# Ordering the loads of a background weight preparation behind the stores of y

## The chip, the core and the metric

The kernel runs on one core of a Trainium2 chip. The metric is the device time of one execution in microseconds (us). Five engines work side by side, each taking its own instructions in order: PE (TensorE, matrix products), DVE (VectorE), ACT (ScalarE), POOL (GpSimd) and SP (SyncE), which in this kernel does nothing but issue DMAs, all of them. They meet through semaphores.

## What is computed

One decoder layer on a sequence of 2048 tokens of width 1024, in float32. In the reference, shortened:

```
u = rmsnorm(x, norm_mix)
z = u @ w_in                                  # 1024 -> 5392
aq, ak, av, gq, gk, gv, g_low, za, zg = split(z)
y_att = sliding_window_attention(rope(aq), rope(ak), av, sinks)      # 16 heads, 2 kv heads, window 128
log_g = log_sigmoid(g_low @ w_gate_up + b_gate) / 16
o     = gated_linear_attention(gq, gk, gv, log_g)                    # 4 heads, chunks of 64
y = concat(y_att * silu(za), rmsnorm(o, gla_norm) * silu(zg)) @ w_out    # 2048 -> 1024
h = x + y
h = h + sigmoid(rmsnorm(h, ple_norm) @ w_ple_gate) * (p @ w_ple_proj)
return rmsnorm(h, final_norm)
```

## The kernel before

Each float32 operand is split into a high and a low part, and a product is three passes of PE: high by high, high by low, low by high (`gemm`, L83).

**First phase** (L126 to L734). It runs in two halves of 1024 tokens. A half begins with a section over its eight blocks of 128 tokens: keys, values and the low-rank gate input (`section_a`), and one behind it the first block of GLA values (`v_block`). Then come four rounds `i`, one GLA head each: eight `v_block`s (in round 0 they have been done in the section), two pairs of `qk_block`s, eight `gla_tile`s; and behind them attention for two, one, one and no groups of four heads, each with eight `att_tile`s and four `za_block`s. Round 3 has no attention. `load_w` brings the weights of each block; in the first half it converts them (ACT copies the high part, POOL subtracts, L286 and L288) and stores the parts, in the second half it loads the stored parts (`wh`, `wl`, L278 and L279).

Every tile ends in a store to the array `yts` (called y below), from `oy` by attention (L480) and from `oyg` by GLA (L587).

The tails of these tiles are generators in a list `chains`. `tick()` advances each of them by one step; it is called behind each block, and `run_chain` runs a tile's first part, ticks and appends the tile.

**The right operands.** The second phase (L739 to the end) multiplies y by `w_out` in two passes, and the normalised result by `w_ple_gate`, by a scheme of seven products in place of eight on blocks of a 2 by 2 cut. Its right operands are seven combinations of each pass's weight blocks, each split in high and low. `right_operands` (L595) makes them while the first phase runs, as one of the chains, in 48 units (3 passes, 4 × 4 blocks). A unit takes four loads of 64 KB of raw rows (`rb`, L605), four differences on DVE (`tm`, by `diff`, L104), two copies on ACT (`th`, L621), two subtractions on POOL (L622) and four stores to `tds` (L624). A unit's loads stand in the code two units ahead of its differences. All of it lives in the nine buffers of the pool `rawp`, tag `raw`.

In round 3 of half 1, behind the `v_block`s, the pools of keys, values and raw rows are closed, the pool `tpr` takes their place (its tiles wait for the buffers they overlap) and the first three of the seven operands `T` are loaded (L122).

**What sets the order.** The program is written in one order, but a scheduler arranges each engine's instructions by its own model of time: among those that are ready it takes the one that stands first in the code. So an instruction that has nothing to wait for may be issued far ahead of its place in the code. A load of raw rows waits for a free buffer of `rawp` and nothing else.

Of the kernel before, what the change touches and what calls it, by code (L numbers as in the profile page):

```python
# [19 lines left out]
P = 128  # L20
# [18 lines left out]
def hybrid_block_kernel(  # L39
# [86 lines left out]
    with ExitStack() as p1:  # L126
# [181 lines left out]
        def tick():  # L308
            for c in list(chains):
                if next(c, True):  # L310
                    chains.remove(c)

        def spawn(c):
            chains.append(c)
# [94 lines left out]
        def att_tile(half, g, wq, lt, szas):  # L409
            kv = g // 2  # L410
            t = half * HT + lt
            ps = pt("acc")
            tok_gemm(ps, wq, lt, 0, 256)
            q = w1("q", shape=(P, 4, 64))
            act.activation(q, ps[:, 0:256].rearrange("p (h d) -> p h d", h=4), AF.Copy)
            rope(q, 4, t)
            stk = w2("stk", F32R, (P, 4, 2, 64))
            split(stk[:, :, 0, :], stk[:, :, 1, :], q)
            yield
            tp = pt("t", dtype=F32R)  # L420
            for j in range(4):
                pe.transpose(tp[:, j * P:(j + 1) * P], stk[:, j].rearrange("p a d -> p (a d)"), identr)
            qT = w2("qT", F32R, (P, 4, P))
            act.activation(qT, tp.rearrange("p (h n) -> p h n", h=4), AF.Copy)
            yield
            sp = pt("s", (P, 4, 256), bufs=1)
            win = slice(lt * P, lt * P + 256)
            for j in range(4):
                pe.matmul(sp[:, j, :], qT[:, j, :], kT[:, kv, 0, win], start=True, stop=False)
                pe.matmul(sp[:, j, :], qT[:, j, :], kT[:, kv, 1, win], start=False, stop=True)  # L430
            s = w2("s", F32, (P, 4, P))
            act.activation(s, sp[:, :, P:256], AF.Copy)
            um = umask.unsqueeze(1).broadcast_to([P, 4, P])
            if t == 0:
                dve.copy_predicated(s, um, negc.unsqueeze(2).broadcast_to([P, 4, P]))
            else:
                dve.copy_predicated(s, um, sp[:, :, 0:P])
            hsl = slice(4 * g, 4 * g + 4)
            sm = wk.tile([P, 6, 4], F32, name="sm", tag="sm", bufs=3)
            mx, ng, es, su, dn = (sm[:, i, :] for i in range(5))  # L440
            dve.tensor_reduce(out=mx, in_=s, op=ALU.max, axis=AX.X)
            dve.scalar_tensor_tensor(ng, mx, -1.0, nsk[:, hsl], op0=ALU.mult, op1=ALU.min)  # L442
            dve.tensor_tensor(es, ng, nsk[:, hsl], op=ALU.subtract)
            act.activation(es, es, AF.Exp)
            for j in range(4):
                act.activation(s[:, j, :], s[:, j, :], AF.Exp, bias=ng[:, j:j + 1], accum_out=su[:, j:j + 1])  # L446
            dve.tensor_tensor(dn, su, es, op=ALU.add)
            dve.reciprocal(dn, dn)
            dve.scalar_tensor_tensor(s, s, 0.5, dn.unsqueeze(2).broadcast_to([P, 4, P]),
                                     op0=ALU.mult, op1=ALU.mult)  # L450
            yield
            yield
            tp = pt("t")
            for j in range(4):
                pe.transpose(tp[:, j * P:(j + 1) * P], s[:, j, :], ident)
            pq = kvp.tile([P, 4, 512], F32R, name="pq", tag="pq", bufs=1)
            split(pq[:, 0, :], pq[:, 1, :], tp)
            pmb = pmask.unsqueeze(1).broadcast_to([P, 4, P])
            for i in range(2):
                pool.tensor_tensor(pq[:, 2 + i, :].rearrange("p (h n) -> p h n", h=4),  # L460
                                   pq[:, i, :].rearrange("p (h n) -> p h n", h=4), pmb, op=ALU.mult)
            yield
            yield
            po = pt("o")
            vp = vs[:, lt, kv].rearrange("p a d -> p (a d)")
            vq = vd[:, lt, kv].rearrange("p a d -> p (a d)")
            pe.matmul(po, vp, pq[:, 0, :], start=True, stop=False)
            pe.matmul(po, vp, pq[:, 1, :], start=False, stop=False)
            pe.matmul(po, vq, pq[:, 2, :], start=False, stop=False)
            pe.matmul(po, vq, pq[:, 3, :], start=False, stop=True)  # L470
            pv = po.rearrange("p (a b n) -> p a b n", a=2, b=2)
            ot = w1("ot", shape=(P, 2, P))
            act.activation(ot[0:64], pv[64:128, :, 0, :], AF.Copy)
            act.activation(ot[64:128], pv[0:64, :, 1, :], AF.Copy)
            dve.tensor_tensor(ot[0:64], ot[0:64], pv[0:64, :, 0, :], op=ALU.add)
            dve.tensor_tensor(ot[64:128], ot[64:128], pv[64:128, :, 1, :], op=ALU.add)
            oy = w1("oy", shape=(P, 2, P))
            l2 = lt % 4
            dve.tensor_tensor(oy, ot, szas[lt // 4][:, :, l2 * P:(l2 + 1) * P], op=ALU.mult)
            nc.sync.dma_start(yts[t][:, 2 * g:2 * g + 2, :], oy)  # L480


        def gla_gates(half, h, sub, res):
# [65 lines left out]
        def gla_tile(half, h, wz, lt, ops):  # L549
            t = half * HT + lt  # L550
            if t > 0:
                sd = w1("sd")
                dve.tensor_scalar(sd, st[:, h, :], dall[:, h, t - 1, 1:2], dall[:, h, t, 0:1],
                                  op0=ALU.mult, op1=ALU.mult)
                sh = w2("sh", F32R, (P, 2, 256))
                split(sh[:, 0], sh[:, 1], sd)
            yield
            kt, at, qq, vv = ops[lt]
            ps = pt("acc")
            tok_gemm(ps, wz, lt, 0, 256)  # L560
            m = w1("m")
            act.activation(m, ps[:, 0:256], AF.Tanh, scale=0.5)
            dve.scalar_tensor_tensor(m, m, 1.0, ps[:, 0:256], op0=ALU.add, op1=ALU.mult)  # L563
            pool.tensor_tensor(m, m, gn, op=ALU.mult)
            pk = pt("o")
            mm3(pk[:, 0:256], kt, vv, True, True)
            if t > 0:
                dve.tensor_tensor(st[:, h, :], pk[:, 0:256], sd, op=ALU.add)
            else:
                dve.tensor_copy(st[:, h, :], pk[:, 0:256])  # L570
            po = pt("o")
            if t > 0:
                mm3(po[:, 0:256], qq, sh, True, False)
            mm3(po[:, 0:256], at, vv, t == 0, True)
            y = w1("y")
            ss = small.tile([P, 1], F32, name="ss", tag="ss", bufs=4)
            act.activation(y, po[:, 0:256], AF.Square, accum_out=ss)
            rs = rms_scale(ss, 256)
            dve.scalar_tensor_tensor(y, po[:, 0:256], rs, m, op0=ALU.mult, op1=ALU.mult)
            yield  # L580
            yield
            tq = pt("t")
            for j in range(2):
                pe.transpose(tq[:, j * P:(j + 1) * P], y[:, j * P:(j + 1) * P], ident)
            oy = w1("oyg", shape=(P, 2, P))
            act.activation(oy, tq[:, 0:256].rearrange("p (a n) -> p a n", a=2), AF.Copy)
            nc.sync.dma_start(yts[t][:, 8 + 2 * h:10 + 2 * h, :], oy)  # L587

        def run_chain(c):
            next(c)  # L590
# [4 lines left out]
        def right_operands():  # L595
            units = [(ps_, k, c) for ps_ in range(3) for k in range(4) for c in range(4)]

            def piece(name, dtype=F32):
                return rawp.tile([P, 2 * SW], dtype, name=name, tag="raw")[:, 0:512].rearrange("p (b n) -> p b n", b=4)

            def load(ps_, k, c):
                r = piece("rb")

                for i, (kk, a) in enumerate(((0, 1), (0, 0), (1, 0), (1, 1))):
                    nc.sync.dma_start(r[:, i], srcs[ps_][(k + 4 * kk) * P:(k + 4 * kk + 1) * P,  # L605
                                                         512 * a + c * P:512 * a + c * P + P])
                return r

            rs_ = [load(*u) for u in units[:2]]
# [1 line left out]
            for n, (ps_, k, c) in enumerate(units):  # L611
# [15 lines left out]
                if n + 2 < len(units):  # L627
                    rs_.append(load(*units[n + 2]))
                yield
                if n % 3 == 0:  # L630
                    yield

        A_COLS = [(C_AK, 256), (C_GL, 16)]
# [18 lines left out]
        for half in range(2):  # L652
            if half > 0:
                carry_kv()
                spawn(right_operands())
            wv = load_w([(C_GV, 256)])
            vt, gates = {}, {}
            for s_ in range(HT + LAG):
# [16 lines left out]
                if s_ >= LAG:  # L675
                    v_block(wv, vt, s_ - LAG)
                    tick()

            for i in range(4):
                if i > 0:  # L680
# [7 lines left out]
                        tick()  # L688
                if half == 1 and i == 3:

                    kvs.close()
                    p2p["tpr"] = p2r.enter_context(tc.tile_pool(name="tpr", bufs=1, side="right", reuse_waits="tile"))
                    T = [None] * 7
                    load_T(0, ORDER[:3], T)
# [389 lines left out]
```

## Time and profile before

| | us |
|---|---|
| median of 3 runs | 1932.47 |
| lowest and highest | 1930.56, 1933.31 |
| the profiled execution | 1929.69 |
| span of the profiled execution (first to last instruction) | 1927.6 |
| PE busy | 1828.3 (95% of the span) |
| DVE busy | 1224.1 (64%) |
| ACT busy | 962.7 (50%) |
| POOL busy | 697.9 (36%) |
| DMA queue of SP | 324.70 MB, 52.2% of what 16 DMA engines could be busy |
| mean granted clock of PE | 0.981 of full speed |

Times in the profile are counted from the first instruction of the span. A share over the whole span mixes stages with different limits, so the stretches are what is to be read. Matmuls are pipelined and their ends modelled, so a busy PE may still hide gaps that are too short to see. POOL's spans are rough. Idle time of an engine matters only where the engine that sets the end waits for it.

### The profile page before, as it was taken

How to read it: one execution, taken by the hardware profiler on the slowest of the kernel's cores; microseconds unless marked ns; L12 is line 12 of the kernel's file. 1: busy time of each engine (PE TensorE's matmuls, PEld its weight loads, DVE VectorE, ACT ScalarE, POOL GpSimd, SP SyncE). 2: the span in 40 equal slices, each digit the busy share in tenths (PEclk: the TensorE clock that was granted, in tenths of full speed). 3: DMA queues.
4: the chain of work that ended last, by engine and by line, in shares of the span. 5: the costliest groups of instructions: out<-in, count | busy, mean ns of one | idle time of the engine just before them, and what ended most of it. 6: DMA issues, size and time to landing. Idle time of an engine off the chain costs nothing. (4 is left out here: it accounts for less than half of the span.)

```text
span 1927.6 us, 32806 instructions
## 1 busy us (share of the span) xinstructions
PE 1828.3 (95%) x11297; PEld 1626.3 (84%) x11297; DVE 1224.1 (64%) x2663; ACT 962.7 (50%) x2598; POOL 697.9 (36%) x916
## 2 busy tenths in 40 slices
PE   6999999999998888988999999999899999998997
PEld 6989898998998778778898998998788888786886
DVE  6455775475457776657774474475666666766875
ACT  5554665466456565546563464465422234453543
POOL 5452554443526678554332232232200001112322
PEclk9999999999999889999999999999999999999999
DMA  8332442423417998996232231335586876894542
GB/s 278 123 97 80 148 145 78 154 90 130 136 43 227 265 285 248 268 277 184 79 105 77 83 102 58 105 100 185 170 301 192 313 257 209 287 351 145 177 138 92
DMA packets 326741, 326.78 MB, mean 170 GB/s; under 512 B 23136, under 2 KB 259824, under 8 KB 326320
## 3 DMA queue, kind: packets, MB, share of 16 engines
q1 hardware_dynamic: 326576, 324.70, 52.2%
q8 instruction: 89, 1.46, 0.3%
q14 instruction: 76, 0.62, 0.1%
HBM read 186.08 MB, written 138.54 MB: 168 GB/s over the span
## 5 line engine op out<-in xcount | busy, mean ns | idle before, releaser
L85 PE MATMUL acc<-wh,uth 128*128 128x256 f32 (+1 forms) x1664 | 481.3, 290 | 15.1 <-DVE m L563 7.7
L86 PE MATMUL acc<-wl,uth 128*128 128x256 f32 (+1 forms) x1664 | 476.0, 286 | 0.9 <-DMA wl<-wd 0.8
L87 PE MATMUL acc<-wh,utl 128*128 128x256 f32 (+1 forms) x1664 | 475.6, 286 | 0.0
L85 PEld LDWEIGHTS acc<-wh,uth 128*128 128x128 f32 x1664 | 320.4, 193 | 26.7 <-DVE m L563 9.0
L86 PEld LDWEIGHTS acc<-wl,uth 128*128 128x128 f32 x1664 | 320.1, 192 | 6.1 <-DMA wl<-wd 1.5
L87 PEld LDWEIGHTS acc<-wh,utl 128*128 128x128 f32 x1664 | 320.2, 192 | 1.9
L460 POOL TENSOR_TENSOR pq<-pq,pmask 128x512 fp32r<-128x512 f32 x128 | 175.8, 1391 | 387.8 <-ACT pq L67 382.1
L85 PE MATMUL acc<-uth,wh 128*128 128x512 f32 x512 | 205.8, 402 | 3.8 <-DVE m L563 2.7
L87 PE MATMUL acc<-uth,wl 128*128 128x512 f32 x512 | 203.3, 397 | 1.0 <-DMA wl<-wd 1.0
L86 PE MATMUL acc<-utl,wh 128*128 128x512 f32 x512 | 203.8, 398 | 0.0
L768 PE MATMUL acc<-T,c 128*128 128x512 f32 (+1 forms) x344 | 135.0, 394 | 5.0 <-ACT u L823 4.8
L769 PE MATMUL acc<-T,c 128*128 128x512 f32 (+1 forms) x344 | 135.0, 392 | 0.0
L770 PE MATMUL acc<-T,c 128*128 128x512 f32 (+1 forms) x344 | 134.4, 393 | 0.0
L446 ACT ACTIVATE s<-s,sm 128x128 f32<-128x128 f32 x256 | 99.7, 391 | 51.6 <-DVE sm L442 51.3
L85 PEld LDWEIGHTS acc<-uth,wh 128*128 128x128 f32 x512 | 97.5, 190 | 26.0 <-DVE m L563 4.0
L87 PEld LDWEIGHTS acc<-uth,wl 128*128 128x128 f32 x512 | 97.2, 190 | 23.8 <-DMA wl<-wd 1.7
L288 POOL TENSOR_TENSOR wl<-raw,wh 128x512 fp32r<-128x512 f32 (+1 forms) x82 | 109.9, 1370 | 20.2 <-ACT wh L286 10.3
L853 POOL TENSOR_TENSOR ssh<-ssh 128x1 f32<-128x1 f32 x16 | 4.0, 250 | 312.5 <-ACT junk L852 312.5
L86 PEld LDWEIGHTS acc<-utl,wh 128*128 128x128 f32 x512 | 97.3, 190 | 18.9
L768 PE MATMUL o<-T,c 128*128 128x512 f32 (+1 forms) x252 | 98.7, 392 | 1.1 <-DVE xt L107 0.9
L769 PE MATMUL o<-T,c 128*128 128x512 f32 (+1 forms) x252 | 98.0, 389 | 0.0
L770 PE MATMUL o<-T,c 128*128 128x512 f32 (+1 forms) x252 | 97.9, 389 | 0.0
(288 smaller groups left out, 4382.4 us busy)
## 6 DMA issues: line engine op xcount, KB each, us to landing
T<-td SPq DMA_DIRECT2D x84, 512.0 KB, 9.0
wd<-wh SPq DMA_DIRECT2D x20, 1024.0 KB, 5.6
wd<-wl SPq DMA_DIRECT2D x20, 1024.0 KB, 6.4
wh<-wd SPq DMA_DIRECT2D x80, 256.0 KB, 5.4
wl<-wd SPq DMA_DIRECT2D x80, 256.0 KB, 5.6
raw<-in_w_in SPq DMA_DIRECT2D x68, 256.0 KB, 5.6
y<-yts SPq DMA_DIRECT2D x64, 256.0 KB, 6.1
td<-th SPq DMA_DIRECT2D x48, 256.0 KB, 3.0
```

The source lines that it names most:

```text
L85: pe.matmul(ps, lhs_h(k), rhs_h(k), start=(k == 0), stop=False)
L86: pe.matmul(ps, lhs_h(k), rhs_l(k), start=False, stop=False)
L87: pe.matmul(ps, lhs_l(k), rhs_h(k), start=False, stop=(k == nk - 1))
L288: eng.tensor_tensor(wl[:, ks_, 0:n], raw[:, :, 0:n], wh[:, ks_, 0:n], op=ALU.subtract)
L446: act.activation(s[:, j, :], s[:, j, :], AF.Exp, bias=ng[:, j:j + 1], accum_out=su[:, j:j + 1])
L460: pool.tensor_tensor(pq[:, 2 + i, :].rearrange("p (h n) -> p h n", h=4), pq[:, i, :].rearrange("p (h n) -> p h n", h=4), pmb, op=ALU.mult)
L768: pe.matmul(ps, c[:, 0, k, :], t[:, 0, k, sl], start=(first and k == 0), stop=False, skip_group_check=more)
L769: pe.matmul(ps, c[:, 0, k, :], t[:, 1, k, sl], start=False, stop=False, skip_group_check=more)
L770: pe.matmul(ps, c[:, 1, k, :], t[:, 0, k, sl], start=False, stop=(k == 3), skip_group_check=more)
L853: pool.tensor_tensor(ss[:, 0:1], ss[:, 0:1], ss[:, 1:2], op=ALU.add)
```

## The change

It gives the loads of raw rows a place in SP's queue. The instruction of the latest store of y is kept in `pace[0]`, and each unit's four loads are traced under `tc.issue_after(pace[0])`, which adds an order without a semaphore: on the engine of that store (SP) these loads come behind it. The chain is started behind the loop of half 1's section instead of at the start of half 1, it takes an empty tick after every sixth unit instead of every third, and an assert states that it has ended when its pool is closed.

```diff
@@ att_tile
-            nc.sync.dma_start(yts[t][:, 2 * g:2 * g + 2, :], oy)
+            pace[0] = nc.sync.dma_start(yts[t][:, 2 * g:2 * g + 2, :], oy).ins
@@ gla_tile
-            nc.sync.dma_start(yts[t][:, 8 + 2 * h:10 + 2 * h, :], oy)
+            pace[0] = nc.sync.dma_start(yts[t][:, 8 + 2 * h:10 + 2 * h, :], oy).ins
+
+        pace = [None]
@@ right_operands
             def load(ps_, k, c):
                 r = piece("rb")
 
-                for i, (kk, a) in enumerate(((0, 1), (0, 0), (1, 0), (1, 1))):
-                    nc.sync.dma_start(r[:, i], srcs[ps_][(k + 4 * kk) * P:(k + 4 * kk + 1) * P,
-                                                         512 * a + c * P:512 * a + c * P + P])
+                with tc.issue_after(pace[0]):
+                    for i, (kk, a) in enumerate(((0, 1), (0, 0), (1, 0), (1, 1))):
+                        nc.sync.dma_start(r[:, i], srcs[ps_][(k + 4 * kk) * P:(k + 4 * kk + 1) * P,
+                                                             512 * a + c * P:512 * a + c * P + P])
                 return r
...
                 yield
-                if n % 3 == 0:
+                if n % 6 == 0:
                     yield
@@ the two halves
             if half > 0:
                 carry_kv()
-                spawn(right_operands())
...
                     v_block(wv, vt, s_ - LAG)
                     tick()
+            if half == 1:
+                spawn(right_operands())
...
                 if half == 1 and i == 3:
 
+                    assert not any(c.__name__ == "right_operands" for c in chains)
                     kvs.close()
```

## Rows read from the trace of the kernel before

**Rows 1.** Page, 40 equal slices: busy tenths of PE and of the DMA engines.

```profile
PE   6999999999998888988999999999899999998997
...
DMA  8332442423417998996232231335586876894542
```

**Rows 2.** Windows: stretch, length, busy us by engine (instructions), clock, DMA share, GB/s.

```profile
600.00:900.00 300.00, 260.01 (x1679) 234.78 (x1678) 205.31 (x498) 162.59 (x427) 198.85 (x267) 0.92 0.88 256
1000.00:1300.00 300.00, 298.04 (x2087) 274.94 (x2086) 169.07 (x421) 148.32 (x457) 82.61 (x113) 1.00 0.27 85
250.00:550.00 300.00, 292.61 (x2044) 269.17 (x2044) 176.50 (x411) 164.71 (x487) 136.80 (x151) 1.00 0.37 120
...
900.00:1320.00 420.00, 415.94 (x2896) 382.04 (x2896) 256.52 (x639) 223.00 (x691) 121.94 (x141) 1.00 0.28 88
```

**Rows 3.** Tiles rb, tm: ns min/median/max, first and last start us, shapes.

```profile
L605 SPq DMA_DIRECT2D rb<-in_w_out x128: 346/496/1632, 578.5 to 795.0; - x128
L605 SPq DMA_DIRECT2D rb<-in_w_ple_gate x64: 361/489/1278, 796.0 to 889.0; - x64
...
L104 DVE TENSOR_TENSOR tm<-rb x96: 275/289/1387, 589.4 to 892.1; 128x128 f32<-128x128 f32 x96
L104 DVE TENSOR_TENSOR tm<-rb,tm x96: 259/287/1387, 592.2 to 894.0; 128x128 f32<-128x128 f32 x96
...
L622 POOL TENSOR_TENSOR rb<-rb,th x48: 992/1020/1988, 593.1 to 895.4; 128x384 fp32r<-128x384 f32 x48
...
L622 POOL TENSOR_TENSOR tm<-tm,th x48: 1269/1302/2276, 595.4 to 896.5; 128x512 fp32r<-128x512 f32 x48
```

**Rows 4.** Waits of PE, 600 to 900: us in total, times, longest us.

```profile
PE acc L85 <- DVE m L563: 7.1, 4, 3.2
...
PE t L584 <- DVE utl L68: 3.3, 2, 3.1
...
PE t L584 <- DVE y L579: 3.0, 1, 3.0
...
PE t L346 <- DVE gT L397: 1.6, 1, 1.6
PE t L392 <- DVE gT L397: 1.5, 1, 1.5
PE t L392 <- DVE utl L68: 1.4, 2, 0.7
```

**Rows 5.** Waits of DVE, 570 to 900, for raw rows.

```profile
DVE tm L104 <- DMA rb<-in_w_out: 21.4, 14, 5.9
...
DVE tm L104 <- DMA rb<-in_w_ple_gate: 6.6, 4, 3.7
```

**Rows 6.** Windows: a short stretch within the block.

```profile
648.70:655.50 6.80, 5.83 (x20) 5.05 (x21) 6.80 (x17) 4.13 (x13) 4.89 (x7) 0.50 0.91 245
```

**Rows 7.** Line 513, first qk operation of each GLA head and quarter, from 700.

```profile
L513 DVE SCALAR_TENSOR_TENSOR qk<-acc,e x8: 678/691/693, 778.3 to 1347.9; 128x512 f32<-128x512 f32 x8
```

**Rows 8.** Lines 122 (1300 to 1350) and 768: loads of T, products with T.

```profile
L122 SPq DMA_DIRECT2D T<-td x12: 359/549/1067, 1319.3 to 1331.7; - x12
...
L768 PE MATMUL acc<-T,c x344: 277/389/796, 1376.9 to 1915.7; 128*128 128x512 f32 x170, 128*128 128x256 f32 x2
```

**Rows 9.** Groups of DVE, 578 to 898: busy us, mean ns, idle before.

```profile
L104 DVE TENSOR_TENSOR tm<-rb 128x128 f32<-128x128 f32 x96 | 41.0, 448 | 20.5 <-DMA rb<-in_w_out 9.6 <-DMA rb<-in_w_ple_gate 6.3 <-POOL pq L460 3.1
L104 DVE TENSOR_TENSOR tm<-rb,tm 128x128 f32<-128x128 f32 x96 | 38.3, 399 | 13.1 <-DMA rb<-in_w_out 11.7 <-DMA rb<-in_w_ple_gate 0.3
```

**Rows 10.** Groups of POOL, 250 to 550: conversion of weights.

```profile
L288 POOL TENSOR_TENSOR wl<-raw,wh 128x512 fp32r<-128x512 f32 x40 | 52.5, 1344 | 10.8 <-PE t L584 9.7 <-ACT wh L286 0.9
```

**Rows 11.** Waits of SP, whole span.

```profile
SPq L480 <- DVE oy L479: 321.5, 42, 30.6
```

**Rows 12.** Tile wl, 778 to 1330: its loads.

```profile
L279 SPq DMA_DIRECT2D wl<-wd x69: 359/460/987, 777.9 to 1318.8; - x69
```

**Rows 13.** Waits of PE, whole span, for a weight.

```profile
PE acc L87 <- DMA wl<-wd: 1.0, 1, 1.0
```

## Prediction

> **What bounds the kernel now.** I read the slices of the page first [rows 1]. TensorE (PE) is busy nearly everywhere, so only stretches where it is not can give anything. Besides the first and last slices, which the change doesn't touch, one block stands out: in slices 13 to 19 PE falls to 8 and 9 tenths and the DMA engines go up to 9. I then cut that block out and set it beside two others of 300 us that run GLA and attention tiles as well [rows 2]. From 600 to 900 us PE is busy 260.0 of 300 us at a mean granted clock of 0.92; in the undisturbed part of half 1, 1000 to 1300 us, 298.0 us at 1.00; in half 0, 250 to 550 us, 292.6 us at 1.00.
>
> What lives in the block is the preparation of the right operands. All its 192 loads start between 578.5 and 889.0 us, its last subtraction at 896.5 us [rows 3]. So 48 units that the code hands out over some 113 ticks run in 320 us, 6.7 us each, because nothing but a free raw buffer holds their loads back. Meanwhile PE waits for things that VectorE (DVE) and ScalarE (ACT) deliver late: `m`, `utl`, `y`, `gT` [rows 4]. DVE in its turn stood 28.0 us (21.4 + 6.6, 18 times) before a difference `tm` until its raw rows had landed [rows 5]. DVE takes its instructions in order, so a `tm` whose rows are late holds up the `m` or `y` behind it. The clock goes too: PE's single wait of 3.0 us for `y` [rows 4] lies at the head of a stretch of 6.8 us that was granted 0.50, 1.2 of 2.4 GHz [rows 6].
>
> The price of the block: idle 300 − 260.0 = 40 us, and clock (1 − 0.92) × 300 = 24 us, together **64 us**, or 64 / 48 = 1.33 us a unit.
>
> **The change part by part.** No instruction is added or removed: 192 load issues, 192 differences, 96 ACT copies, 96 POOL subtractions and 192 stores are all moved. The assert is Python's. Two edits only set the calendar: the chain is started behind the loop over keys, values and the first v blocks of half 1 instead of ahead of it, and its empty ticks come every 6 units instead of every 3. Counted in ticks: 1 for the first loads, 2 × 48, and 8 empty ones, 105. From the end of that loop to the opening of the pool of `T` there are 36 + 32 + 32 + 8 = 108. The work fits, with 3 ticks to spare.
>
> *What the pacing does.* The edge from the last store of y to a load is an order on SP's queue and no semaphore: a unit's four loads cannot stand ahead of that store. Stores of y come all through half 1's GLA and attention tiles. So the loads, and the rest behind them, spread from about 778 us, where half 1's first `qk` block ends its section of keys and values [rows 7], to about 1320 us, where `T` is opened [rows 8]: 542 us, 11.3 us a unit, 5.0 us a tick. The first three or four units have only a store of half 0 ahead of them and may still come earlier.
>
> *Removed: the burst.* 600 to 778 us loses its foreign work. What PE then loses there is shown by no row, as half 1's section ran only under the burst. The nearest row is half 0's rate, 7.4 us in 300 [rows 2], so 178 us lose 4.4 us. The ends: at the rate of the quiet stretch 2.0 / 300 × 178 = 1.2 us; if the waits on the section's own `utl` and `gT` (3.3 + 1.6 + 1.5 + 1.4, [rows 4]) all stay, 7.8 us. I take 4.4. The 122 us from 778 to 900, without the burst, lose 0.8 us at the quiet rate. Removed: 64 − 4.4 − 0.8 = **58.8 us**.
>
> *Put back: the same units, spread (R).* Shares over 900 to 1320 us [rows 2] plus the moved work over 542 us: DVE 256.5 / 420 = 0.61, plus 79 us of differences (41.0 + 38.3, [rows 9]) / 542 = 0.15, makes 0.76. POOL 121.9 / 420 = 0.29, plus 48 × (1.02 + 1.30) = 111 us [rows 3], 0.21, makes 0.50. DMA 0.28 plus (0.88 − 0.28) × 300 / 542 = 0.33, makes 0.61, against 0.88 now. Nothing is full, but DVE is fuller than in the burst (205.3 / 300 = 0.68). PE's loss is bounded from both sides by rows. Below: half 0 has similar extra work, 40 POOL subtractions `wl` of 1.34 us in 300 us with their ACT copies [rows 10], and loses 7.4 − 2.0 = 5.4 us more than the quiet stretch, 0.135 us for each; 96 of them make 13 us. (A gain is excluded but for some 4 us: the stretch that takes the work loses no more now.) Above: the full price of the burst, 64 us. I take **20 us**, 0.42 us a unit: near the lower row, since POOL stands as in half 0 (136.8 / 300 = 0.46 there, 0.50 here) and the DMA engines are far from full, but above it for the differences on DVE, which half 0 hasn't.
>
> *The wait that comes in.* SP stood 321.5 us in all before the stores from `oy`, 30.6 us at the longest [rows 11]. Behind such a store now stand four loads, and behind them the unit's stores, weight loads and further stores of y. Who waits for the loads is DVE's `tm`, placed four ticks later in the code, some 20 us, unless the scheduler fills a gap of DVE with it sooner. Price: between nothing and the 28 us that DVE now waits for raw rows; it is inside R. The issues themselves cost nothing while SP has little but waits to do.
>
> *The end.* `T` takes the room of the raw buffers. Its first 12 loads are now issued from 1319.3 to 1331.7 us; the first product with `T` starts at 1376.9 us [rows 8]. The preparation will end some 3 ticks ahead of them instead of 420 us ahead. The cover is 1376.9 − 1331.7 = 45 us less the landing of the last. I cost it at nothing; beyond that each us of lateness is a us of the end.
>
> *Sum.* 58.8 − 20 = 38.8 us. The profiled execution took 1929.7 us (its span and 2.1 us around it); the median of the runs is 1932.5, 2.8 us more. 1929.7 − 38.8 + 2.8 = **1894 us**. Its own range: R = 13 and 1.2 us in the vacated stretch give a gain of 64 − 1.2 − 0.8 − 13 = 49, 1883 us, and a few us less if gaps too short for the view go too; R = 40 and 7.8 us give 64 − 7.8 − 0.8 − 40 = 15, 1917 us.
>
> **Rivals.**
>
> *Longer differences keep their price.* 96 of the differences took 448 ns in the mean, the 96 others 399 [rows 9], and the shortest of either 275 and 259 [rows 3]: 96 × 173 + 96 × 140 ns = 30 us of DVE time, with single ones of 1387 ns. If that belongs to the unit and not to the burst, and each us reaches PE because DVE is then 0.76 full, R = 13 + 30 = 43 and the gain is 58.8 − 43 = 16 us: **1917 us**. For it: a POOL subtraction takes about as long as the longest exceed the shortest. Against: attention keeps several ticks between DVE's results and PE's use of them.
> The Trainium skill, page "SBUF — State Buffer", section "SBUF: two separate sides", has a rule for this: VectorE and GpSimd share one pair of ports as an exclusive lock, and a VectorE operation with two SBUF inputs is blocked for the whole of a GpSimd operation that began first. By that rule spreading saves nothing of these 30 us, since every difference still has two SBUF inputs; the 1387 ns here agree with it.
>
> *The burst's price travels.* Either the scheduler still packs units (where no new store of y comes for some ticks, as at the start of each group of GLA tiles, several units hang on one store), or DVE meets late rows as often as now: 1.33 us a unit. Then R = 64, and the gain is 58.8 − 64 = −5: **1937 us**. This is also what would come out if the edges didn't do what they say and the block merely moved by 100 us or more. For it: DVE's 18 waits for raw rows came with two units loaded ahead, and still are. Against: half 0 carries like work at 2 × 0.135 = 0.27 us for each two subtractions, a fifth of that price.
>
> *Weights held up behind the queue (slower).* From 778 us to the end of attention 69 issues of `wl`, four to a load, make 17 loads of weights [rows 12], all on SP's queue. If each found a unit's eight issues of about 0.49 us [rows 3] ahead of it, it would be 3.9 us late, 17 × 3.9 = 66 us, and the gain turns into 38.8 − 66 = −27: **1960 us**. It decides from 38.8 / 17 = 2.3 us per load. For it: PE already waits for `wl` at times, 1.0 us at the longest [rows 13], so some loads have no margin. Against: weights are loaded in the burst too, with preparation twice as dense, and the waits that lead there name DVE and ACT [rows 4].
>
> **How the numbers follow.** Forecast 0.74 (1880 to 1917), longer differences 0.11 (1917), price travels 0.09 (1928 to 1942), weights 0.06 (1945 to 1965). About 0.2%, 3.9 us, is what a measurement of this kernel can tell from no change. Faster by more: 0.74 + 0.11 = 0.85; within it: 0.05, the near part of the third; slower: 0.04 + 0.06 = 0.10. The range reaches from 1872 (the low end of the forecast and some more for the short gaps) to 1920, which takes in the second case and leaves out the last two and a tail.
>
> **What would show it.** Right: loads of `rb` from about 720 or 780 to 1320 us; PE at clock 1.00 and above 48 of 50 us in each stretch from 600 to 780; a DMA share of about 0.6, level up to 1320; PE's idle time in what is now 778 to 1320 at about 20 us above the quiet rate; half 1's first `qk` block, now at 778.3 us, some 25 to 30 us earlier. Wrong: DVE waiting over 28 us for `rb`; a mean `tm` above 400 ns with PE waiting on `m` and `pq`; PE waits that name `wl` or `wh`; the first product with `T` later than 1376.9 less what was gained before it; half-clock stretches behind 900 us.

## The result and the profile after

The changed kernel takes 1904.6 us (median of 4 runs, 1903.7 to 1906.2), the kernel before 1932.9 us beside it: a ratio of **0.9854**, with an interval of 0.9837 to 0.9872. That is 28.3 us less; 38.5 us less were forecast, and the time lies in the range. The profiled execution has a span of 1902.3 us.

The slices of the page (40 equal ones: busy tenths of PE, granted clock of PE, busy tenths of the DMA engines) answer to [rows 1]:

```profile
PE   6999999999999999999999999999899999998997
...
PEclk9999999999999999999999999999999999999998
...
DMA  8332442415324352655576566565685966884542
```

The hole in slices 13 to 19 is gone, and the hill of the DMA engines with it; in its place there is a plateau of 5 to 7 tenths from slice 17 to slice 28. The windows (stretch, length, busy us of PE, PE's weight loads, DVE, ACT and POOL with instructions, granted clock, DMA share, GB/s) say the same in numbers, beside [rows 2]:

```profile
600.00:900.00 300.00, 290.32 (x2025) 265.08 (x2025) 181.86 (x472) 159.69 (x466) 132.39 (x211) 1.00 0.46 143
1000.00:1300.00 300.00, 286.52 (x1970) 261.64 (x1970) 192.45 (x497) 162.18 (x481) 140.64 (x152) 0.99 0.63 185
250.00:550.00 300.00, 292.66 (x2042) 269.07 (x2041) 176.01 (x410) 165.53 (x491) 135.91 (x151) 1.00 0.37 120
900.00:1320.00 420.00, 396.92 (x2702) 360.43 (x2702) 271.99 (x694) 232.77 (x681) 197.71 (x209) 0.99 0.64 191
744.00:1294.00 550.00, 525.73 (x3576) 476.84 (x3575) 363.18 (x946) 306.15 (x908) 260.64 (x276) 0.99 0.60 177
```

From 600 to 900 us PE is busy 290.3 us instead of 260.0, at clock 1.00 instead of 0.92. But from 1000 to 1300 us it is busy 286.5 instead of 298.0: part of the price has moved there. The tiles of the preparation and the ends of the rounds (ns min/median/max, first and last start in us), to [rows 3, 7, 8]:

```profile
L609 SPq DMA_DIRECT2D rb<-in_w_out x128: 328/436/1721, 695.5 to 1080.8; - x128
L609 SPq DMA_DIRECT2D rb<-in_w_ple_gate x64: 327/440/1317, 1093.9 to 1264.8; - x64
...
L626 POOL TENSOR_TENSOR tm<-tm,th x48: 1264/1298/2198, 704.9 to 1273.0; 128x512 fp32r<-128x512 f32 x48
```

```profile
L513 DVE SCALAR_TENSOR_TENSOR qk<-acc,e x8: 676/692/692, 743.7 to 1321.6; 128x512 f32<-128x512 f32 x8
```

```profile
L774 PE MATMUL acc<-T,c x344: 281/389/796, 1350.5 to 1883.1; 128*128 128x512 f32 x170, 128*128 128x256 f32 x2
```

The loads run from 695.5 to 1264.8 us, 11.9 us a unit. The first product with `T` starts at 1350.5 instead of 1376.9 us, 26.4 us earlier, and from there to the end of the span both kernels take 551 to 552 us: in these two traces, whose spans differ by 25.3 us, the whole gain lies in the first phase. PE's waits from 744 to 1294 us (us in total, times, longest us):

```profile
PE acc L86 <- DMA wl<-wd: 6.0, 7, 2.5
PE o L525 <- ACT sh L67: 4.4, 4, 2.5
PE acc L85 <- DMA wh<-wd: 2.8, 5, 0.9
PE acc L85 <- ACT v L522: 2.7, 2, 2.1
PE acc L85 <- DVE m L563: 2.0, 4, 1.1
PE o L525 <- ACT kt L67: 2.0, 2, 1.8
```

The wait for `y` of [rows 4] is no longer there, and `m` is down from 7.1 to 2.0 us. `utl` and `gT` belong to the section, which lies ahead of this window; from 600 us on they are 1.9 us in all, where [rows 4] has 7.8. At the head now stand weights, 9.1 us with a smaller row (0.3), which in the whole kernel before were 2.0 us.

### The profile page after: what moved, and what is told of

Read it like the earlier page. It is cut to its first block, busy times and chain, and to the rows that moved or that the text cites. A ratio compares the mean times of both kernels' runs of the same rounds, so it can differ in the third digit from the quotient of the medians.

```text
span 1902.3 us, 32715 instructions
## 1 busy us (share of the span) xinstructions
PE 1814.7 (95%) x11297; PEld 1612.9 (85%) x11297; DVE 1203.3 (63%) x2663; ACT 961.1 (51%) x2598; POOL 699.3 (37%) x916
## 3 DMA queue, kind: packets, MB, share of 16 engines
q8 instruction: 89, 1.46, 0.3%
## 5 line engine op out<-in xcount | busy, mean ns | idle before, releaser
L85 PEld LDWEIGHTS acc<-wh,uth 128*128 128x128 f32 x1664 | 316.0, 190 | 25.6 <-ACT v L522 5.9
L86 PEld LDWEIGHTS acc<-wl,uth 128*128 128x128 f32 x1664 | 315.7, 190 | 12.9 <-DMA wl<-wd 8.6
L87 PEld LDWEIGHTS acc<-wh,utl 128*128 128x128 f32 x1664 | 315.7, 190 | 2.0
L87 PEld LDWEIGHTS acc<-uth,wl 128*128 128x128 f32 x512 | 96.1, 188 | 22.5 <-DMA wl<-wd 0.7
L67 ACT ACTIVATE c<-s 128x512 fp32r<-128x512 f32 x72 | 45.1, 629 | 111.1 <-DVE s L104 32.4
L774 PE MATMUL o<-T,c 128*128 128x512 f32 (+1 forms) x252 | 99.3, 394 | 0.0
L775 PE MATMUL o<-T,c 128*128 128x512 f32 (+1 forms) x252 | 98.6, 391 | 0.0
```

Of the source, the lines that this page charges most:

```text
L67: act.activation(h, src, AF.Copy)
L85: pe.matmul(ps, lhs_h(k), rhs_h(k), start=(k == 0), stop=False)
L86: pe.matmul(ps, lhs_h(k), rhs_l(k), start=False, stop=False)
L87: pe.matmul(ps, lhs_l(k), rhs_h(k), start=False, stop=(k == nk - 1))
L774: pe.matmul(ps, c[:, 0, k, :], t[:, 0, k, sl], start=(first and k == 0), stop=False, skip_group_check=more)
L775: pe.matmul(ps, c[:, 0, k, :], t[:, 1, k, sl], start=False, stop=False, skip_group_check=more)
```

## The experiments

Each run's ratio stands against runs of the kernel before on the same chip. For the comparisons between runs I turn ratios into us on the 1932.9 of above; where a median of the run itself is given, it is called one. Line numbers of a kernel shift by a few with its edit.

### Which part of the change does it: e1, e2

e1 takes the order away and keeps the calendar, e2 the reverse.

```diff
@@ e1, on the changed kernel
-                with tc.issue_after(pace[0]):
+                if True:
@@ e2, on the changed kernel
-            if half == 1:
-                spawn(right_operands())
...
                 carry_kv()
+                spawn(right_operands())
...
-                if n % 6 == 0:
+                if n % 3 == 0:
```

> The changed kernel with the later start and the sparser empty ticks, but without the order behind the stores of y. Theory (it is the order in SP's queue that spreads the work): the loads are hoisted again as soon as buffers are free, they start near 578 us as before, and the time is 1926 to 1936 us. Rival (the calendar does it: a later place in the code is enough): loads start near 700 us and end near 1270 us as in the changed kernel, 1902 to 1910 us.

> The changed kernel with the order behind the stores of y, but the start and the empty ticks of the kernel before (start at the head of half 1, an empty tick every 3 units). Theory: the spread is kept, except that some 7 units of the section of keys and values hang on the last store of half 0 and run there as a small burst at 1.3 us each; half 1's later part has as many units fewer: 1903 to 1912 us. Rival (calendar): 1926 to 1936 us.

e1: 0.9993 (0.9982 to 1.0003), no change. Its tile view shows why:

```profile
L609 SPq DMA_DIRECT2D rb<-in_w_out x128: 424/496/1396, 579.1 to 794.4; - x128
L609 SPq DMA_DIRECT2D rb<-in_w_ple_gate x64: 345/484/1607, 795.4 to 889.7; - x64
```

These are the times of the kernel before within 1 us, though the units stand some 16 ticks later in the code: a load that waits for a free buffer alone goes out whenever there is one. e2: 0.9848 (0.9829 to 0.9867), a median of 1904.7 us, the time of the changed kernel. So the order behind the stores of y is all of the gain, and the calendar is worth nothing that these runs can see.

### What the spread preparation still costs: e3

e3 leaves the whole preparation out. `T` is then loaded in the same pieces from the stored parts of `w_in`, which `wlist()` gives, so the second phase multiplies other numbers.

```diff
@@ e3, on the changed kernel
-            if half == 1:
-                spawn(right_operands())
...
-                nc.sync.dma_start(T[i][:, :, k, :].bitcast(F32), tds[ps_][:, i, :, k, :])
+                nc.sync.dma_start(T[i][:, :, k, :].bitcast(F32),
+                                  wlist()[i][:, :, 2 * k:2 * k + 2, :].rearrange("p a b n -> p a (b n)"))
```

> The changed kernel without any preparation of right operands; T is loaded in the same pieces from stored parts of w_in instead, so the second phase multiplies other numbers. It measures what the spread preparation still costs. By the profile of the changed kernel PE idles 26.7 us from 744 to 1349 us and loses some 6 us to the clock, against some 4 us at the quiet rate, so the preparation costs 29 us there: 1872 to 1879 us. If later stages take back what is saved (T loaded sooner, the same waits in the second phase), 1880 to 1895 us. If the price had been the forecast 20 us: 1885 us.

0.9645 (0.9629 to 0.9661), a median of 1865.5 us. So the preparation costs 69 us as a burst and 40 us spread, (1 − 0.9645) and (0.9854 − 0.9645) of 1932.9, and not the 29 us that idle time and clock had led to expect. The stages tell where. The table is worked out from the first starts of `qk` in each round (the rows of line 513, of which one stands above for the last 8 of 16) and the start of the first product with `T`; in brackets the units whose loads start in the stage:

| us | before | changed | e3 | e4 | e10 |
|---|---|---|---|---|---|
| half 0, round 2 to 3 | 160.5 (6) | 153.2 | 153.1 | 153.3 | 153.2 |
| half 0, round 3, and half 1's section | 151.9 (22.5) | 125.4 (3) | 125.2 | 127.4 (6) | 124.5 |
| half 1, round 0 | 244.3 (19.5) | 230.4 (18) | 217.6 | 271.5 (37) | 230.4 |
| half 1, round 1 | 149.5 | 153.9 (14) | 149.3 | 159.1 (5) | 151.8 |
| half 1, round 2 | 149.6 | 166.0 (13) | 149.5 | 149.6 | 153.0 |
| half 1, round 3, to the first product with `T` | 55.2 | 56.5 | 55.2 | 55.2 | 55.2 |

Against e3 the kernel before pays 7.4 + 26.7 + 26.7 us in the three stages where the burst runs. The changed kernel pays nothing in the first two and 12.8 + 4.6 + 16.5 + 1.3 = 35 us behind them. Some 3 us more lie behind the first product with `T`, from where the changed kernel takes 551.8 us to the end of the span and e3, with its other numbers, 549.0. The windows of rounds 0 to 2 show how busy the engines are (for the changed kernel the one from 744 to 1294 us above; here e3):

```profile
744.00:1260.00 516.00, 512.94 (x3573) 472.17 (x3572) 305.37 (x762) 263.08 (x816) 146.47 (x184) 1.00 0.27 84
```

The same matmuls (3576 and 3573) take 550 and 516 us. And yet, PE aside, no engine is busy more than 0.66 of the stretch (DVE, 363.2 / 550), POOL 0.47, DMA 0.60. Of the 34 us, 21 are idle time of PE (24.3 us, in e3 3.1). The other 13 lie in PE's busy time, 525.7 against 512.9 us, though the matmuls are the same. The clock accounts for some 3.4 of these, an estimate: half of two stretches of 3.4 us each that were granted 0.50, 1.2 of 2.4 GHz, the first behind the wait of 2.5 us shown further below:

```profile
933.40:936.80 3.40, 3.40 (x16) 3.30 (x17) 2.52 (x9) 0.63 (x2) 0.83 (x1) 0.50 1.09 362
1145.00:1148.40 3.40, 3.40 (x16) 3.18 (x16) 3.40 (x8) 3.38 (x10) 2.79 (x5) 0.50 0.87 244
```

What the rest is made of no run here shows.

### Does the price follow the density: e4

One tick a unit, so that 48 units are nearly as close as in the burst, but each still behind its store:

```diff
@@ e4, on the changed kernel
-                    if i0 == 0:
-                        yield
...
-                if n % 6 == 0:
-                    yield
```

> The changed kernel with one tick a unit instead of two and a sixth, so that 48 units take some 50 ticks (about 270 us, 5.6 us a unit, as close as in the kernel before), still behind the stores of y. If the price of a unit follows density (queues filled by neighbours): 1.3 us a unit, 1932 to 1942 us. If it follows the unit alone (0.6 us, as in the changed kernel): 1902 to 1910 us.

1.0023 (1.0013 to 1.0033): slower than the kernel before. The loads run from 696.6 to 1049.0 us, 7.3 us a unit, and round 0, with 37 units, takes 54 us more than without any. In its window (746 to 1018 us) the clock is 0.94:

```profile
746.00:1018.00 272.00, 238.46 (x1496) 210.81 (x1495) 197.67 (x489) 150.00 (x434) 152.29 (x146) 0.94 0.76 219
```

54 / 37 = 1.46 us a unit, against 61 / 48 = 1.27 in the kernel before and 35 / 48 = 0.73 in the changed one. The order behind the stores is no gain by itself; what counts is the distance between units that it keeps. The mean distance does not set the price alone, though: in the changed kernel a unit costs 12.8 / 18 = 0.71 us in round 0, 4.6 / 14 = 0.33 in round 1 and 16.5 / 13 = 1.27 in round 2, at 12.8, 11.0 and 12.8 us a unit. How the units lie within a round matters as well; a lump of them in round 2 is shown below.

### What in a unit costs it: e7 to e10

e7 leaves out POOL's subtractions, e8 DVE's differences, e9 the stores, e10 all that is not a DMA.

```diff
@@ e7, on the changed kernel
-                    pool.tensor_tensor(src.bitcast(F32R), src, h, op=ALU.subtract)
@@ e8, on the changed kernel
-                tm = piece("tm")
-                diff(dve, tm[:, 1], r[:, 0], r[:, 1])
...
-                for src, i0, m in ((r[:, 1:4], 0, 3), (tm, 3, 4)):
+                for src, i0, m in ((r, 3, 4), (r[:, 1:4], 0, 3)):
...
@@ e9, with T loaded as in e3
-                    for j, part in enumerate((h.bitcast(F32), src)):
-                        nc.sync.dma_start(tds[ps_][:, i0:i0 + m, j, k, c * P:(c + 1) * P], part)
@@ e10, with T loaded as in e3, in place of differences, copies and subtractions
+                for src, i0, m in ((r[:, 1:4], 0, 3), (r, 3, 4)):
+                    for j in range(2):
+                        nc.sync.dma_start(tds[ps_][:, i0:i0 + m, j, k, c * P:(c + 1) * P], src)
```

> The changed kernel without the 96 POOL subtractions of the preparation; the raw values are stored in place of the low parts. If POOL, or its sharing of a port with DVE, carries much of the 39 us that the preparation still costs (1904.6 against 1865.5 without it), 15 us or more go: 1880 to 1890 us, and the mean of the differences falls from 360 and 313 ns to near 280. If not: 1897 to 1906 us. A stay of the lengthened differences with no gain in time would tell against the rule of the shared pair as a term of the sum.

> The changed kernel without the 192 differences of the preparation; ACT and POOL take the raw rows themselves, and the four-block part goes first. If the load on DVE (64 us, a share of 0.1) carries the cost, 15 us or more go: 1880 to 1890 us. If the DMAs and their order carry it, little: 1896 to 1906 us.

> The changed kernel without the 192 stores of the preparation (loads, differences, copies and subtractions stay); T is loaded from stored parts of w_in, as in e3, so the second phase multiplies other numbers. Without any preparation the time was 1865.5 us, with all of it 1904.6: 39 us. Leaving out DVE's part gave 7 us, POOL's 5. If the stores (43 MB, half of the unit's issues on SP, three quarters of its bytes) carry the rest, 1870 to 1882 us. If engines that wait for late rows carry it, 1890 to 1902 us.

> The reverse of e9: all 384 DMAs of the preparation with their shapes, none of its differences, copies and subtractions; raw rows are stored in place of the parts, and T is loaded as in e3. If SP's queue and the DMA engines carry the cost, 1890 to 1902 us; if DVE, ACT and POOL together do (each of them alone being replaceable), 1868 to 1880 us.

| | ratio (interval) | what is left of the 40 us | of the 35 us of the stages |
|---|---|---|---|
| e7, no subtractions | 0.9822 (0.9801 to 0.9844) | 34 | 27 |
| e8, no differences | 0.9815 (0.9791 to 0.9839) | 33 | 27 |
| e9, no stores | 0.9792 (0.9769 to 0.9816) | 28 | 30 |
| e10, DMAs alone | 0.9741 (0.9722 to 0.9760) | 19 | 18 |

No single one of these parts carries the price; e7 and e8 end in the cases of little gain, and their intervals still overlap that of the changed kernel (0.9837 to 0.9872). No run leaves out ACT's copies alone. In e7 the differences didn't get shorter either. Groups of DVE (busy us, mean ns, idle time before), first of the changed kernel, 690 to 1300 us, to [rows 9], then of e7, 570 to 1300 us:

```profile
L104 DVE TENSOR_TENSOR tm<-rb 128x128 f32<-128x128 f32 x96 | 31.8, 360 | 19.5 <-DMA rb<-in_w_ple_gate 9.0 <-DMA rb<-in_w_out 7.8 <-POOL tm L626 2.2
L104 DVE TENSOR_TENSOR tm<-rb,tm 128x128 f32<-128x128 f32 x96 | 30.0, 313 | 2.9 <-DMA rb<-in_w_out 1.1 <-DMA rb<-in_w_ple_gate 0.9
```

```profile
L104 DVE TENSOR_TENSOR tm<-rb 128x128 f32<-128x128 f32 x96 | 30.6, 345 | 32.4 <-DMA rb<-in_w_ple_gate 16.2 <-DMA rb<-in_w_out 14.0 <-DMA td<-th 1.7
L104 DVE TENSOR_TENSOR tm<-rb,tm 128x128 f32<-128x128 f32 x96 | 30.5, 318 | 0.9
```

In e9 the stores, half of a unit's issues and three quarters of its bytes, carry 12 us by the ratios and 5 by the stages, not most of the price; behind the first product with `T`, e9 and e10 multiply other numbers as e3 does, in 549.7 and 547.9 us to the end. e10 lies between its two cases: it pays 19 us with the DMAs alone. By the table of stages, e10 pays 12.8 us in round 0, as much as the changed kernel, but 2.5 and 3.5 us in rounds 1 and 2, against 4.6 and 16.5. So the DMAs by themselves don't make the price of round 2. That they make that of round 0 is not shown: e7 and e8 have the same DMAs and pay only 5.3 and 5.5 us there (stages of 223.0 and 223.1 us), and e10 has a wait in SP's queue that the changed kernel hasn't, its stores waiting for the landing of raw rows (690 to 1300 us):

```profile
SPq L624 <- DMA rb<-in_w_out: 27.7, 24, 3.2
SPq L624 <- DMA rb<-in_w_ple_gate: 10.7, 11, 1.7
```

What happens in SP's queue can be seen where PE waits longest for a weight in the changed kernel (SP from 917 to 931 us: start, length, line, DMA):

```profile
922.75 0.36 SPq L278 DMA_DIRECT2D wh<-wd  x1
923.53 0.33 SPq L480 DMA_DIRECT2D yts<-oy  x1
923.92 2.97 SPq L609 DMA_DIRECT2D rb<-in_w_out  x4
926.99 0.38 SPq L628 DMA_DIRECT2D td<-th  x1
927.46 0.43 SPq L279 DMA_DIRECT2D wl<-wd  x1
```

and PE:

```profile
931.47 0.38 PE L86 MATMUL acc<-wl,uth 128*128 128x256 f32 x1 [2.53 <-DMA wl<-wd]
```

The `wl` of a load follows its `wh` by 4.7 us, where 0.5 us is usual; between them stand a store of y, a unit's four loads and a store of the preparation. PE goes on 4.0 us after its issue, having stood for 2.5 us. In round 2 several units hang on one store: after a store at 1132.9 us, the loads of four units and sixteen stores of the preparation go through SP's queue by 1156 us (the expectation of e5, below, counts five units). ACT has stood for 9 us before a copy whose rows were among them, behind it on ACT comes a copy `kt` of GLA, and PE waits 1.8 us for that (start, length, and idle time before):

```profile
1140.46 0.52 ACT L625 ACTIVATE th<-rb 128x384 fp32r<-128x384 f32 x1 [9.00 <-DMA rb<-in_w_ple_gate]
1141.11 0.63 ACT L625 ACTIVATE th<-tm 128x512 fp32r<-128x512 f32 x1
1141.64 0.26 ACT L67 ACTIVATE kt<-t 128x128 fp32r<-128x128 f32 x1
1141.95 0.38 PE L525 MATMUL o<-vv,kt 128*128 128x256 f32 x1 [1.78 <-ACT kt L67]
```

The first operation `qk` of the round's second pair of blocks comes 35.4 us behind that of the first (1128.0, 1163.4), in e3 26.2 us. In e10 the loads of four units go through the queue behind one store there too (1131.0 to 1145.8 us), and it is 26.2 us (1127.5, 1153.7); in e7, e8 and e9, which all keep ACT's copies, it is 30.9, 33.4 and 32.3 us. So at this place the lump costs time only with the engines' part, and leaving out POOL's, DVE's or the stores takes some of it away, but none of them all.

### Two attempts at the waits: e5, e6

e5 lets the loads also wait for their turn behind weights; e6 fixes the place of the differences and copies among DVE's and ACT's instructions.

```diff
@@ e5, load_w, on the changed kernel
-                    nc.sync.dma_start(wl[:, ks_, 0:n].bitcast(F32), saved[:, 1, ks_, :])
+                    pace[0] = nc.sync.dma_start(wl[:, ks_, 0:n].bitcast(F32), saved[:, 1, ks_, :]).ins
@@ e6, right_operands, on the changed kernel (held: the last result of y on DVE, on ACT)
+                with tc.issue_after(held[0]):
...
+                    with tc.issue_after(held[1]):
```

> The changed kernel, with the loads of raw rows queued behind the latest load of weights as well as behind the latest store of y (pace[0] is also set by load_w). In the changed kernel PE waits 9.1 us from 744 to 1294 us for weights that stand behind a unit's issues in SP's queue, and where no store of y comes for some ticks, several units follow on one store (five from 1133 to 1156 us). Theory (the order on SP's queue carries a good part of what the preparation still costs): these waits go and the lumps thin out, 1888 to 1899 us. Rival (late raw rows, not late weights, carry it; rows behind weights are later still): 1902 to 1912 us.

> The changed kernel, with the differences queued on DVE behind the latest result of y, and the copies on ACT behind the latest copy for y, so that the scheduler cannot pull them ahead of their place in the code to where their rows have only just been asked for. In the changed kernel DVE sat 18.9 us and ACT 23.4 us idle before them until raw rows landed, and PE waits some 9 us more for sh, kt, m and v than without preparation. Theory (late rows in front of in-order engines carry a good part): these idle times fall below 5 us each and the time to 1890 to 1899 us. Rival (engines have slack for it): 1901 to 1908 us.

e5: 0.9861 (0.9839 to 0.9883), the time of the changed kernel, and so in the rival's range. PE still waits 7.9 us for weights (4.5 + 2.7 + 0.7); a unit's four stores and the stores of y, which the edit leaves where they were, can still stand among them. So the waits did not go this way, and how much they cost by themselves stays open.

e6: 0.9959 (0.9946 to 0.9973), 20 us worse than the changed kernel and outside both cases. Idle time before the differences and copies until raw rows had landed fell from 42.3 us (18.9 + 23.4) to 20.1 us, less than expected, and PE paid for it elsewhere. Its longest wait, from 1305 to 1380 us:

```profile
PE acc L86 <- DMA wl<-wd: 7.8, 1, 7.8
```

The units end later; their last store leaves SP at 1299.7 us, and the twelve loads of `T` go out from 1302.8 us on, the last eight within 9.3 us. Behind them stands the rest of a load of weights, issued from 1316.3 us. Here a single wait for weights is twice the 3.9 us that the prediction's rival put on a load, in another kernel than the one it was written for.

### A longer stretch: e11, e12

e11 starts in half 0's round 3, at 2.75 ticks a unit; e12 also loads raw rows three units ahead.

```diff
@@ e11, on the changed kernel
-            if half == 1:
-                spawn(right_operands())
...
                 wz = load_w([(C_ZG + 256 * i, 256)])
+                if half == 0 and i == 3:
+                    spawn(right_operands())
...
-                if n % 6 == 0:
+                if n % 4:
@@ e12, on e11
-            rs_ = [load(*u) for u in units[:2]]
+            rs_ = [load(*u) for u in units[:3]]
...
-                if n + 2 < len(units):
-                    rs_.append(load(*units[n + 2]))
+                if n + 3 < len(units):
+                    rs_.append(load(*units[n + 3]))
```

> The changed kernel with a longer stretch for the preparation: it starts in round 3 of half 0, behind the load of its last weights, and a unit takes 2.75 ticks, so that some 10 units lie ahead of half 1's rounds. The prices so far: about 1.3 us a unit at 6 us a unit (before, e4), 0.8 us at 11 us a unit. If price follows density, about 0.6 us at some 14 us a unit: 29 us in place of 39, 1892 to 1899 us. If units in the section of keys and values, which hang on one store, are dearer than those they replace: 1904 to 1912 us.

> e11 with the raw rows of a unit loaded three units ahead of its differences instead of two. In e11 DVE still sat 19.1 us and ACT 15.6 us idle before the preparation's instructions until raw rows had landed. If late rows at the head of in-order engines carry the cost, these waits fall by half or more and the time to 0.976 to 0.980 of the kernel before (1888 to 1895 us). If not (the ninth buffer runs out, or the scheduler places the differences right behind the landing however early that is), 0.980 to 0.984 (1896 to 1903 us).

e11: 0.9814 (0.9793 to 0.9835), 1897 us. Its stages take 11.8 + 4.8 + 7.7 + 5.7 + 1.0 = 31 us more than e3's, 0.65 us a unit, at 621.1 / 48 = 12.9 us a unit (loads from 620.6 to 1241.7 us): the case of a price that follows density. e12: 0.9797 (0.9784 to 0.9811), 1894 us, the fastest kernel here that still computes the layer; the intervals of both lie below that of the changed kernel, but that of e12 not below that of e11. In e12 DVE no longer waits for raw rows at all and ACT 7.9 us (19.1 and 15.6 in e11). The time falls by 3 us, to the edge of the first case, but no further from e11 than the runs can tell; ACT's waits before the same copies now mostly name stores of the preparation that have not freed a buffer (20.0 us in all, 14.3 in e11). The longest rows of e12:

```profile
ACT th L625 <- DMA td<-th: 11.5, 4, 5.1
ACT th L625 <- DMA td<-tm: 7.5, 4, 3.4
ACT th L625 <- DMA rb<-in_w_out: 7.1, 2, 6.5
```

So that late raw rows carry the whole of the remaining price is not shown, here or in e6: idle time of DVE or ACT that was taken away in one place came back, at least in part, in another.

## Why the prediction was right, and where it was off

- **What bounds the kernel: right.** The block from 600 to 900 us was priced at 64 us from idle time and clock; against e3 the three stages of the burst lose 61 us, by the ratios 69. e1 shows that a free buffer was all that had held the loads back.
- **Removed, 58.8 us: right within some us in the traces,** which give 61; the ratios give 69. The vacated stage takes 125.4 us, in e3 125.2: nothing of the burst is left there. What that stage loses of itself is 6.2 us (e3: PE busy 118.8 of 125 us from 619 to 744), where 4.4 us were put in.
- **R, the price of the spread units: this term was mis-sized,** 20 us where 40 are measured by the ratios and 35 in the traces. The step that failed is the choice near the lower bound, by the shares and by idle time. The shares came out as forecast or lower (DVE 0.66 for 0.76, POOL 0.47 for 0.50, DMA 0.60 for 0.61), and still the price was nearly double. PE's idle time came out as forecast as well, 21 us above e3's, but 13 us more lie in its busy time, where the reckoning from rows had no term but the clock. The lower bound of 13 us priced a POOL subtraction with its copy; e10 has none of either and pays 19 us. The DMAs of a unit, and their place in SP's queue, were not in the bound. Shares of a stretch say nothing of what an instruction that comes late holds up behind it in order, as the copy `kt` on ACT shows.
- **The sum: in the range, in part by luck.** In the traces it reads 61 − 35 = 26 us instead of 58.8 − 20 = 38.8, and the miss is R's. By the ratios it is 69 − 40 = 28 us once rounding is left out: 10 us more removed than was put in offset half of what R lacked.
- **The wait that comes in: inside R, as said, but not its seat.** DVE's waits for raw rows fell from 28.0 to 18.9 us, and e12, on a longer stretch, took them away for some 3 us, which its runs can't tell from nothing.
- **The calendar: right, and not needed.** The count of ticks holds (the work ended ahead of `T`); the prediction gave the calendar no price, and e2 does without it.
- **The end, at nothing: right.** The first product follows round 3's first `qk` by 1.3 us more than in e3. That lateness there costs was shown by e6.
- **Rival, longer differences: no.** They got shorter without POOL or DVE losing work: spread, they take 96 × (360 − 274) + 96 × (313 − 263) ns = 13 us over the shortest, where the burst had 30. Without the preparation's subtractions (e7) the means are 345 and 318 ns, so these subtractions are not what lengthens the rest. The Trainium skill, page "SBUF — State Buffer", section "SBUF: two separate sides", has VectorE and GpSimd lock each other out of a shared pair of ports, also where a VectorE operation with two SBUF inputs meets a GpSimd operation that reads SBUF. The prediction took from it that the differences would keep their length. The single ones of 1381 ns agree with a lock, and POOL's other work could still cause it, but as a term of this sum the measurement decides against it.
- **Rival, the price travels: no at 11.9 us a unit, yes at 7.3** (e4). The reason given against it, the price of like work in half 0 (0.27 us for two subtractions), did not hold: a unit costs 0.73 us. What kept the price down is, by e4, the distance between the units.
- **Rival, weights behind the queue: the mechanism is there,** 9.1 us of PE's waits instead of 2.0, but far from 3.9 us on every load: most loads have a margin.
- **The signs: mixed.** PE's idle time, the DMA share and the place of the loads came out nearly as said. Two signs of being wrong came too, waits for `wl` and `wh` and, briefly, half clock behind 900 us, and from 600 to 700 us PE is below 48 of 50 us (47.75 and 46.47).

What stays open: the kernel with the DMAs alone pays 19 of the 40 us, with another spread over the rounds. Leaving out POOL's part, DVE's or the stores gives back 6 to 12 us by the ratios, of which only that of the stores is clear of the noise, and 5 to 8 us by the stages. ACT's copies were not left out by themselves, and which meeting of instructions costs what was not settled.

## What to carry to other kernels

Here a background task whose loads waited for nothing but a free buffer ran as a burst, whatever its place in the code. Where you find one that shares an in-order queue with the main work, hang its loads on events of the main work, and measure the price at two or three densities. Price such a task by leaving it out (one run), not by the idle shares of the engines that it uses, nor by PE's idle time alone. When the time of a wait is moved, look next at what else stands in the same queue: weights here came late behind loads that nobody was in a hurry for.

## What was not expected of the hardware

With no engine besides PE busy more than two thirds of the time and the DMA engines at 0.60, the added work still cost PE 34 us in 550 (744 to 1294 us, against 516 in e3). The clock played a small part in it: 0.99 in that window, where the burst had 0.92; in e4's closer units it was down to 0.94 again.
